# Moving the reload of a residual stream and the loads of a post-processing in a fused two-layer encoder

## The chip, the cores and the metric

The kernel runs on one core of a Trainium2 chip. The metric is the device time of one execution in microseconds (us); smaller is better. A core has several engines that run their own instruction streams side by side and wait for each other by semaphores: TensorE (PE: matmuls; PEld: the loading of their weights), VectorE (DVE), ScalarE (ACT, "Activation"), GpSimd (POOL), and SyncE (SP), which here only issues transfers. Transfers between the chip's memory and the on-chip buffers are issued by SP and by ACT, each on a queue of its own and in its own program's order; 16 DMA engines carry them. Float32 is used throughout, and each large product is computed as three products of a high and a low part.

## What is computed

The reference is a stream of 1024 positions of width 1024 through two layers, each followed by a SwiGLU feed-forward block, with a last RMS norm:

```python
def reference(x, ...):
    h = x
    for layer in range(DEPTH):
        hn = rms_norm(h, mix_norm[layer])
        if layer % 2 == 0:
            h = h + hybrid_ab_mixer(hn, ...)
        else:
            y, v_first = rwkv7_time_mix(hn, ...)
            h = h + y
        h = h + swiglu(rms_norm(h, ffn_norm[layer]), ffn_w_gate[layer], ffn_w_up[layer],
                       ffn_w_down[layer])
    return rms_norm(h, final_norm)

def swiglu(hn, w_gate, w_up, w_down):
    return (jax.nn.silu(hn @ w_gate) * (hn @ w_up)) @ w_down
```

The second layer's mixer, `rwkv7_time_mix`, projects the stream to r, k, v, a decay and a gate g, runs a recurrence over time for 16 heads of 64 channels, and ends with a post-processing: a group norm of the recurrence's result y, a bonus term that multiplies v, and the gate:

```python
    y = wkv7_scan(rh, decay, kh, vh, -kk, kk * ah)
    mean = jnp.mean(y, axis=-1, keepdims=True)
    var = jnp.mean(jnp.square(y - mean), axis=-1, keepdims=True)
    y = ((y - mean) * lax.rsqrt(var + GN_EPS)).reshape(bsz, seq, d)
    y = y * ln_w.astype(f32) + ln_b.astype(f32)
    bonus = jnp.sum(rh * kh * r_k.astype(f32), axis=-1, keepdims=True) * vh
    y = (y + bonus.reshape(bsz, seq, d)).astype(h.dtype)
    return (y * g) @ w_o, v_first
```

The recurrence is computed in chunks of 64 positions, whose triangular systems are inverted beforehand.

## The kernel before

The sequence is worked on in two halves of 512 positions (`HT`), h = 0 and h = 1. The residual stream of a half is a tile `H[h]` of 128 x 8 x 512 values (2 MB): channels on the partitions in 8 blocks. Memory on the chip is short, so `H[h]` is written to DRAM (`h_d`) and loaded again when the half's turn comes.

**Weights.** `plan` lists all weight tiles of 512 KB in the order in which they are taken. `take(key)` (L133) hands out the next one, counts it in `pos[0]`, has the next two loaded by `load_at` (L108, the issue on ACT's queue at L115) and the next one split by `split` (L144: ACT copies the high part, L145, and DVE subtracts for the low part, L146). Three raw tiles are buffered.

**The two mixed stages.** In each half's turn there is a stage in which the recurrence of one half, `recur` (L1144), runs beside the feed-forward block of the other, `ffn` (L647). Both are generators; `drive` (L731) runs the dense one, earns `RATIO` = 3.0 units for each weight (one eighth of a weight at a time) and spends them on steps of the recurrence, each of which names its cost as it yields. The steps are traced at a priority raised by `AHEAD` = 450 instructions; a scheduler then puts each engine's instructions into a fixed order, by priority and by when it takes them to be ready. So the place of an instruction in the code isn't its place in its engine's stream. `tc.issue_after(i)` draws an edge: what is traced under it stands behind i on i's engine. It adds an order, not a semaphore wait.

**The recurrence's loads.** `load(c)` (L1181) loads what chunk c needs, on SP's queue: `ar` and `bk` (512 KB each), the values `uv`, and the inverses `XT` (L1195, L1198) from `xi_d`, which the stage before has written (L1126). Chunks 0 and 1 are loaded at the start; `burst(c)` (L1269) loads chunk c + 2 at its end. `gram` (L1203) makes the products of `ar` and `bk`, which DVE evicts (L1215); `below`, `below2` and `own` go on with them (evictions L1241, L1255, L1256, L1266), and the state's steps follow. After each second chunk `post(jj)` (L1328) does the post-processing of 128 positions: it loads the gate `gch` (L1332, 512 KB) and the values `vch` (L1335, two loads of 256 KB) on SP's queue, multiplies the values by the bonus (L1341), takes the statistics, normalizes (L1362), applies weight and bonus (L1367, L1368), transposes, applies bias and gate (L1382) and writes the result to `y_d` (L1386). `gch`, `vch` and the rest have one buffer each. Their loads may be scheduled as soon as the buffer is free, long before the steps that use them.

**The residual's reload.** In a mixed stage `with_reload` (L1468) wraps `recur`: while it passes on the recurrence's first four steps it issues the four pieces of the residual (two channel blocks, 512 KB each) on SP's queue (L1474). They are first needed at the first down projection, whose results DVE adds to `H[h]` (L423).

Of the kernel before, what the change touches and what calls it, by code (L numbers as in the profile page):

```python
# [16 lines left out]
P = 128  # L17
D = 1024
T = 1024
KT = D // P  # L20
# [18 lines left out]
def tile_trunk(  # L39
# [8 lines left out]
    act, dve, pool, pe, sp = nc.scalar, nc.vector, nc.gpsimd, nc.tensor, nc.sync  # L48
# [25 lines left out]
    def bc(ap, shape):  # L74
        return ap.to_broadcast(shape)
# [20 lines left out]
    def col(c):  # L96
        return vec[:, c : c + 1]
# [3 lines left out]
    plan, raws, ready, pos = [], {}, {}, [0]  # L101

    acts, dests, splits = set(), {}, {}

    def push(key, parts, view=lambda t: t, dest=None):
        plan.append((key, parts, view, dest))

    def load_at(i):  # L108
        if i >= len(plan) or i in raws:
            return  # L110
        if plan[i][0][0] in acts and plan[i][0][0] not in dests:
            return
        raw = wst.tile([P, D], F32, tag="raw", name="raw")
        for dst, src in plan[i][1]:
            act.dma_start(dst(raw), src)  # L115
        raws[i] = raw

    def whl():
# [197 lines left out]
    H = [hA, hB]  # L316
# [8 lines left out]
    def pst(tag):  # L325
        t, n = psum["tags"][tag]
        return psum["pool"].tile([P, HT], F32, tag=t, bufs=n, name=t)
# [12 lines left out]
    def hsl(h):  # L340
        return slice(h * HT, (h + 1) * HT)
# [6 lines left out]
    def rsqrt(t):  # L348
        pool.tensor_tensor(out=t, in0=t, in1=mhalf[:, : t.shape[1]], op=ALU.pow)  # L349
# [149 lines left out]
    for h in range(2):  # L499
        ops = [mmt() for _ in range(4)]  # L500
        for kp in range(4):
# [4 lines left out]
            for kk in range(2):  # L506
                k = 2 * kp + kk
# [60 lines left out]
    for m in ORD_Z:  # L568
# [4 lines left out]
        for h in range(2):  # L573
# [16 lines left out]
            while w < win:  # L590
                n = l0.tile([P, 16 + HT], F32, tag="zw", bufs=2, name="zw")
                b0 = base + w
# [23 lines left out]
    for h in range(2):  # L616
        hi, lo = act_tiles((xlp, actp)[h])
        ys.append((hi, lo))
        for k in (4, 5, 6, 7, 0, 1, 2, 3):
            src = zt[k - 4, h] if k >= 4 else mx[:, k, hsl(h)]  # L620
# [133 lines left out]
    v_d = [dram.tile([HT, 2, 8, 64], F32, name=f"v_d{h}") for h in range(2)]  # L754
    bon_d = [dram.tile([4, P, 2, 8], F32, name=f"bon_d{h}") for h in range(2)]
    g_d = [dram.tile([P, KT, HT], F32, name=f"g_d{h}") for h in range(2)]
    xi_d = [dram.tile([2, 8, 2, 8, 32, 2, 32], F32, name=f"xi_d{h}") for h in range(2)]
# [31 lines left out]
    rows = [slice(0, 64), slice(64, 128)]  # L789
# [354 lines left out]
    def recur(h, wp):  # L1144
# [5 lines left out]
        def wt(tag, bufs, shape):  # L1150
            return wp.tile(shape, F32, tag=tag, bufs=bufs, name=tag)
# [5 lines left out]
        for r in range(2):  # L1157
            act.dma_start(
                lnw[rows[r]], rwkv_ln_w[0].rearrange("(p r d) -> r p d", r=2, d=64)[r].partition_broadcast(64)
            )  # L1160
        C, ypair = {}, {}
        S, Q, last = [state_d], {}, []

        def ordered(f, *args, **kw):

            if last:
                with tc.issue_after(last.pop()):
                    i = f(*args, **kw)  # L1168
            else:
                i = f(*args, **kw)  # L1170
            last.append(i.ins)
# [9 lines left out]
        def load(c):  # L1181
            ar = wt("ar", 2, [P, 8, 2, 64])
            sp.dma_start(ar, ar_d[h][c])
            bk = wt("bk", 1, [P, 8, 2, 64])
            sp.dma_start(bk, bk_d[h][c])
            uv = wt("uv", 2, [P, 8, 2, 64])
            vs = v_d[h][c * 64 : c * 64 + 64]
            sp.dma_start(uv[64:128, :, 0, :], vs[:, 0])
            sp.dma_start(uv[0:64, :, 1, :], vs[:, 1])

            xx = wt("XT", 2, [P, 8, 96])
            x1, XT = xx[:, :, 0:32], xx[:, :, 32:96]
            for r in range(2):
                b0 = r * 64
                sp.dma_start(  # L1195
                    xx[b0 : b0 + 32, :, 0:64], xi_d[h][0, :, r, c].rearrange("p i a j -> i p (a j)")
                )
                sp.dma_start(XT[b0 + 32 : b0 + 64, :, 32:64], xi_d[h][1, :, r, c, :, 1].rearrange("p i j -> i p j"))  # L1198
                pool.memset(XT[b0 + 32 : b0 + 64, :, 0:32], 0.0)
            gt = wt("gt", 2, [P, 8, 2, P])  # L1200
            C[c] = (ar, bk, uv, gt, x1, XT)

        def gram(c, q):  # L1203
            ar, bk, _, gt, _, _ = C[c]
            og = [pst("sm").rearrange("p (a b) -> p a b", b=P) for _ in range(2)]
            for j in range(4):
                p = q * 4 + j
                for b in range(2):
                    for r in range(2):
                        mm(  # L1210
                            og[r][rows[b], j, :], bk[rows[r], p, b, :],
                            ar[rows[r], p].rearrange("p a b -> p (a b)"), start=True, stop=True,
                        )
            for r in range(2):
                dve.tensor_tensor(  # L1215
                    out=gt[:, q * 4 : q * 4 + 4, r, :], in0=og[r], in1=bc(gm.unsqueeze(1), [P, 4, P]), op=ALU.mult
                )
# [110 lines left out]
        def post(jj):  # L1328
            yp = ypair[0]
            j = h * 4 + jj  # L1330
            gch = wt("gch", 1, [P, 8, P])
            sp.dma_start(gch, g_d[h][:, :, jj * P : (jj + 1) * P])  # L1332
            vch = wt("vch", 1, [P, 2, 8, 64])
            for r in range(2):
                sp.dma_start(  # L1335
                    vch[rows[r]].rearrange("t c p d -> t c (p d)"),
                    v_d[h][jj * P : (jj + 1) * P, r].rearrange("(c t) p d -> t c (p d)", t=64),
                )
            v16 = vch.rearrange("t c p d -> t (c p) d")
            b16 = bon[:, 2 * j : 2 * j + 2, :].rearrange("t c p -> t (c p)")  # L1340
            pool.tensor_tensor(out=v16, in0=v16, in1=bc(b16.unsqueeze(2), [P, 16, 64]), op=ALU.mult)  # L1341
            st = wt("st", 1, [P, 2, 8, 6])
            for r in range(2):
                for p in range(8):
                    dve.bn_stats(out=st[:, r, p, :], in_=yp[:, r, p, :])
            sts = st.rearrange("p a b s -> p (a b) s")
            mean, dm, var = (wt(n, 1, [P, 16]) for n in ("mean", "dm", "var"))
            me, mo, ve, vo = (sts[:, :, i] for i in (1, 4, 2, 5))
            dve.tensor_tensor(out=mean, in0=me, in1=mo, op=ALU.add)
            dve.tensor_tensor(out=dm, in0=me, in1=mo, op=ALU.subtract)  # L1350
            dve.tensor_tensor(out=var, in0=ve, in1=vo, op=ALU.add)
            dve.scalar_tensor_tensor(out=dm, in0=dm, scalar=16.0, in1=dm, op0=ALU.mult, op1=ALU.mult)
            dve.tensor_tensor(out=var, in0=var, in1=dm, op=ALU.add)
            dve.tensor_scalar(out=var, in0=var, scalar1=1.0 / 64, scalar2=GN_EPS, op0=ALU.mult, op1=ALU.add)
            rsqrt(var)
            dve.scalar_tensor_tensor(out=mean, in0=mean, scalar=-0.5, in1=var, op0=ALU.mult, op1=ALU.mult)
            yield 0.3
            ysb = wt("ysb", 1, [P, 2, 8, 64])
            for r in range(2):
                for p in range(8):  # L1360
                    i = r * 8 + p
                    act.activation(  # L1362
                        ysb[:, r, p, :], yp[:, r, p, :], AF.Identity, scale=var[:, i : i + 1], bias=mean[:, i : i + 1]
                    )
            yield 0.3
            for q, eng in enumerate((dve, pool)):
                eng.tensor_tensor(out=ysb[:, q], in0=ysb[:, q], in1=lnw, op=ALU.mult)  # L1367
                eng.tensor_tensor(out=ysb[:, q], in0=ysb[:, q], in1=vch[:, q], op=ALU.add)  # L1368
            yield 0.3
            yield 0.3  # L1370
            for q in range(2):
                o = pst("sm")
                for i in range(4):
                    p = 4 * q + i // 2 * 2
                    ordered(
                        pe.transpose, o[:, i * P : (i + 1) * P], ysb[:, i % 2, p : p + 2, :].rearrange("t p d -> t (p d)"), ident
                    )
                ov = o.rearrange("p (q c r t) -> p q r c t", q=2, c=2, r=2)
                for i in range(4):
                    m = q * 4 + i  # L1380
                    g = gch[:, m, :].rearrange("p (c t) -> p c t", c=2)
                    dve.scalar_tensor_tensor(  # L1382
                        out=g, in0=ov[:, i // 2, i % 2], scalar=col(C_LNB + m), in1=g, op0=ALU.add, op1=ALU.mult,
                    )
                yield 0.5
            sp.dma_start(y_d[h][:, :, jj * P : (jj + 1) * P], gch)  # L1386

        load(0)
        load(1)
        yield 0.2  # L1390
# [77 lines left out]
    def with_reload(pool_, h, src, side):  # L1468

        H[h] = pool_.tile([P, KT, HT], F32, tag="h", name="h")  # L1470
        k = 0
        for cost in side:
            if k < KT:
                sp.dma_start(H[h][:, k : k + 2, :], src[:, k : k + 2, :])  # L1474
                k += 2
            yield cost


# [145 lines left out]
```

## Time and profile before

| what | us |
|---|---|
| median of 3 runs | 2526.85 (2522.3 to 2532.54) |
| profiled execution, own time | 2537.24 |
| its span, first to last instruction | 2535.5 |
| mean granted clock of TensorE | 0.981 of full speed |
| first mixed stage, loads of chunk 0 to the last post-processing's store | 944.58 to 1209.61 |
| second mixed stage, the same | 1690.54 to 1951.07 |

The profile is of one execution. Its page gives the busy time of each engine and the costliest groups of instructions; from the trace behind it one can ask for the timeline of an engine, for waits with what released them, for the chain of waits that ended last, for busy time, granted clock and DMA load in stretches of time, and for the transfers of a queue. "L345" is line 345 of the kernel. Times count from the start of the span. An engine "SPq" or "ACTq" is a transfer being issued on that queue, not the transfer itself. A releaser is inferred from the order of events, so among several awaited things the last one is named. Matmuls are pipelined: their listed durations overlap, and the distance of two starts tells their pace.

### The profile page before, as it was taken

The numbers are of one execution on the slowest core, as the hardware profiler recorded it, in microseconds if no ns is written. First come the engines' busy times: TensorE is split into PE (matmuls) and PEld (weight loads), VectorE is DVE, ScalarE is ACT, GpSimd is POOL, SyncE is SP. The second block draws the span as 40 slices with busy tenths as digits, with TensorE's granted clock in tenths as the row PEclk, the third lists the DMA queues.
The fourth block names the chain that finished last, engine by engine and source line by source line (L and its number), as shares of the span: only waits on it lengthen the run. The fifth ranks groups of instructions, "written<-read, shape, count | busy, mean of one in ns | idle before, by whom it ended". The sixth has DMA issues, their size and how long they took to land.

```text
span 2535.5 us, 37947 instructions
## 1 busy us (share of the span) xinstructions
PE 2443.4 (96%) x15735; PEld 1985.9 (78%) x15735; DVE 1401.2 (55%) x2118; ACT 889.8 (35%) x1335; POOL 298.9 (12%) x298
## 2 busy tenths in 40 slices
PE   8999999999989998999999999899999999999998
PEld 6888888888767776888877677677888878888887
DVE  5446534444865874655457855965654455534443
ACT  6333322222544432333224543432333223322223
POOL 0200000000323400121002222300211000100001
PEclk9999999999989999999999999999999999999999
DMA  5123434323255477533334355585553332423331
GB/s 180 42 60 99 133 109 123 92 92 117 81 156 134 129 204 193 144 104 101 116 119 135 107 180 129 135 222 159 157 149 108 109 100 84 149 83 115 101 92 58
DMA packets 434956, 310.69 MB, mean 123 GB/s; under 512 B 93216, under 2 KB 395424, under 8 KB 433760
## 3 DMA queue, kind: packets, MB, share of 16 engines
q10 hardware_dynamic: 297280, 210.53, 27.9%
q1 hardware_dynamic: 137504, 97.75, 13.7%
q8 instruction: 123, 2.02, 0.3%
q14 instruction: 49, 0.40, 0.1%
HBM read 254.68 MB, written 53.54 MB: 122 GB/s over the span
## 4 chain that ended last, share of the span: by engine, by line
PE 76%; DVE 10%; DMA 8%; ACT 2%; issue 2%; POOL 1%; ACTq 0%; SPq 0%; DVEq 0%; POOLq 0%
PE mm L345 21%; PE mm L344 21%; PE mm L346 21%; PE sm L1168 5%; DVE wlo L146 2%; DMA raw<-in_ffn_w_up_dram 2%; PE yp L1168 1%; DVE mix L887 1%; DVE it L1117 1%; DMA lnw<-in_rwkv_ln_w_dram 1%; DMA raw<-in_ffn_w_down_dram 1%; DVE xi L1122 1%; DMA raw<-n_d 1%; ACT whi L145 1%; DMA raw<-y_d 1%
## 5 line engine op out<-in xcount | busy, mean ns | idle before, releaser
L345 PE MATMUL mm<-alo,whi 128*128 128x512 f32 x1952 | 773.8, 396 | 1.6 <-DVE alo L146 1.6
L344 PE MATMUL mm<-ahi,whi 128*128 128x512 f32 x1952 | 769.0, 395 | 5.0 <-DVE h L423 4.0
L346 PE MATMUL mm<-ahi,wlo 128*128 128x512 f32 x1952 | 767.7, 393 | 2.6 <-DVE wlo L146 2.6
L145 ACT ACTIVATE whi<-raw 128x1024 fp32r<-128x1024 f32 x288 | 304.3, 1058 | 779.5 <-PE mm L345 606.9
L146 DVE TENSOR_TENSOR wlo<-raw,whi 128x1024 fp32r<-128x1024 f32 x288 | 361.4, 1255 | 313.6 <-ACT whi L145 302.7
L344 PEld LDWEIGHTS mm<-ahi,whi 128*128 128x128 f32 x1952 | 368.1, 189 | 92.0 <-issue 4.6
L345 PEld LDWEIGHTS mm<-alo,whi 128*128 128x128 f32 x1952 | 368.7, 189 | 83.7 <-issue 3.7
L346 PEld LDWEIGHTS mm<-ahi,wlo 128*128 128x128 f32 x1952 | 369.0, 189 | 83.2 <-DVE wlo L146 3.4
L345 PE MATMUL mm<-hidlo,wdhi 128*128 128x512 f32 x624 | 248.1, 398 | 1.2 <-DVE hidlo L672 1.2
L344 PE MATMUL mm<-hidhi,wdhi 128*128 128x512 f32 x624 | 240.5, 395 | 6.7 <-ACT hidhi L671 5.5
L346 PE MATMUL mm<-hidhi,wdlo 128*128 128x512 f32 x624 | 246.9, 396 | 0.0
L423 DVE TENSOR_TENSOR h<-h,mm 128x512 f32<-128x512 f32 x192 | 129.6, 686 | 153.8 <-PE mm L346 153.0
L145 ACT ACTIVATE wdhi<-raw 128x1024 fp32r<-128x1024 f32 x82 | 86.6, 1059 | 258.1 <-DMA raw<-in_ffn_w_down_dram 155.2
L146 DVE TENSOR_TENSOR wdlo<-raw,wdhi 128x1024 fp32r<-128x1024 f32 x82 | 101.1, 1234 | 114.6 <-ACT wdhi L145 114.6
L668 DVE TENSOR_TENSOR sg<-sg,mm 128x512 f32<-128x512 f32 x88 | 60.3, 686 | 168.5 <-PE mm L346 168.1
L344 PEld LDWEIGHTS mm<-hidhi,wdhi 128*128 128x128 f32 x624 | 117.8, 189 | 35.0 <-ACT hidhi L671 7.7
L345 PEld LDWEIGHTS mm<-hidlo,wdhi 128*128 128x128 f32 x624 | 119.1, 191 | 28.7 <-DVE hidlo L672 3.2
L346 PEld LDWEIGHTS mm<-hidhi,wdlo 128*128 128x128 f32 x624 | 118.7, 190 | 24.7 <-issue 0.2
L423 DVE TENSOR_TENSOR hA<-hA,mm 128x512 f32<-128x512 f32 x72 | 48.8, 686 | 78.0 <-PE mm L346 78.0
L349 POOL TENSOR_TENSOR nrs<-nrs,small 128x4 f32<-128x4 f32 x8 | 10.0, 1246 | 627.3 <-DVE nrs L371 627.3
L344 PE MATMUL mm<-xhi,whi 128*128 128x512 f32 (+1 forms) x160 | 65.6, 410 | 4.2 <-ACT k L925 4.2
L672 DVE TENSOR_TENSOR hidlo<-sg,hidhi 128x512 fp32r<-128x512 f32 x88 | 65.7, 746 | 3.8 <-ACT hidhi L671 3.7
(300 smaller groups left out, 2948.0 us busy)
## 6 DMA issues: line engine op xcount, KB each, us to landing
raw<-in_ffn_w_gate_dram ACTq DMA_DIRECT2D x88, 512.0 KB
raw<-in_ffn_w_up_dram ACTq DMA_DIRECT2D x88, 512.0 KB
raw<-in_ffn_w_down_dram ACTq DMA_DIRECT2D x88, 512.0 KB
raw<-in_ab_w_in_dram ACTq DMA_DIRECT2D x16, 512.0 KB
raw<-in_ab_w_out_dram ACTq DMA_DIRECT2D x16, 512.0 KB
raw<-in_rwkv_w_k_dram ACTq DMA_DIRECT2D x16, 512.0 KB
raw<-in_rwkv_w_r_dram ACTq DMA_DIRECT2D x16, 512.0 KB
ar_d<-ar SPq DMA_DIRECT2D x16, 512.0 KB
```

The source lines that it names most:

```text
L145: act.activation(hi, src, AF.Copy)
L146: (eng or dve).tensor_tensor(out=lo, in0=src, in1=hi.bitcast(F32), op=ALU.subtract)
L344: pe.matmul(o, whi, xhi, start=first, stop=False)
L345: pe.matmul(o, whi, xlo, start=False, stop=False)
L346: pe.matmul(o, wlo, xhi, start=False, stop=last)
L423: dve.tensor_tensor(out=H[h][:, m, :], in0=H[h][:, m, :], in1=o, op=ALU.add)
L668: dve.tensor_tensor(out=s, in0=s, in1=o, op=ALU.mult)
L672: dve.tensor_tensor(out=lo, in0=s, in1=hi.bitcast(F32), op=ALU.subtract)
L887: dve.scalar_tensor_tensor(out=t, in0=hn1[:, k, 0:HT], scalar=col(c), in1=t, op0=ALU.mult, op1=ALU.add)
L1117: dve.tensor_tensor(out=t, in0=bc(iat[:, j, j + 1 : 32].unsqueeze(2), sh), in1=bc(xi[:, j, 0 : j + 1].unsqueeze(1), sh), op=ALU.mult,)
L1122: dve.tensor_tensor(out=xs, in0=xs, in1=t, op=ALU.add)
L1168: i = f(*args, **kw)
```

## The change

Two things are moved; nothing is computed otherwise, and the same bytes are loaded.

The residual's pieces in `with_reload` go to ACT's queue. A piece is issued only when a new weight has been taken since the piece before (or since the stage's start), and under an edge behind the weight load issued last (`loaded[0]`, which `load_at` now records).

In `post(jj)` the load of the gate gets an edge behind the last `XT` load of a later chunk (`issued[c]`, which `load` now records): chunk 2, 4, 6 and 7 for jj = 0, 1, 2 and 3. The two loads of the values get an edge behind the load of the gate.

```diff
+    loaded = [None]
...
         for dst, src in plan[i][1]:
-            act.dma_start(dst(raw), src)
+            loaded[0] = act.dma_start(dst(raw), src).ins
...
-        C, ypair = {}, {}
+        C, ypair, issued = {}, {}, {}
...
-                sp.dma_start(XT[b0 + 32 : b0 + 64, :, 32:64], xi_d[h][1, :, r, c, :, 1].rearrange("p i j -> i p j"))
+                i = sp.dma_start(XT[b0 + 32 : b0 + 64, :, 32:64], xi_d[h][1, :, r, c, :, 1].rearrange("p i j -> i p j"))
                 pool.memset(XT[b0 + 32 : b0 + 64, :, 0:32], 0.0)
             gt = wt("gt", 2, [P, 8, 2, P])
             C[c] = (ar, bk, uv, gt, x1, XT)
+            issued[c] = i.ins
...
             gch = wt("gch", 1, [P, 8, P])
-            sp.dma_start(gch, g_d[h][:, :, jj * P : (jj + 1) * P])
+            with tc.issue_after(issued[min(2 * jj + 2, 7)]):
+                vload = sp.dma_start(gch, g_d[h][:, :, jj * P : (jj + 1) * P]).ins
             vch = wt("vch", 1, [P, 2, 8, 64])
             for r in range(2):
-                sp.dma_start(
-                    vch[rows[r]].rearrange("t c p d -> t c (p d)"),
-                    v_d[h][jj * P : (jj + 1) * P, r].rearrange("(c t) p d -> t c (p d)", t=64),
-                )
+                with tc.issue_after(vload):
+                    sp.dma_start(
+                        vch[rows[r]].rearrange("t c p d -> t c (p d)"),
+                        v_d[h][jj * P : (jj + 1) * P, r].rearrange("(c t) p d -> t c (p d)", t=64),
+                    )
...
         H[h] = pool_.tile([P, KT, HT], F32, tag="h", name="h")
-        k = 0
+        k, at = 0, pos[0]
         for cost in side:
-            if k < KT:
-                sp.dma_start(H[h][:, k : k + 2, :], src[:, k : k + 2, :])
-                k += 2
+            if k < KT and pos[0] > at:
+                with tc.issue_after(loaded[0]):
+                    act.dma_start(H[h][:, k : k + 2, :], src[:, k : k + 2, :])
+                k, at = k + 2, pos[0]
             yield cost
```

## The prediction

> **What bounds the kernel now.** I read the page first.
>
> ```profile
> span 2535.5 us, 37947 instructions
> PE 2443.4 (96%) x15735; PEld 1985.9 (78%) x15735; DVE 1401.2 (55%) x2118; ACT 889.8 (35%) x1335; POOL 298.9 (12%) x298
> ```
>
> TensorE sets the end. No matmul is added or removed, so the change can only win from the 92.1 us in which PE is idle, and from matmuls at a low clock. The edits lie in the two stages in which a recurrence runs beside a SwiGLU. There I read the waits of PE in the timeline (start, duration, and in brackets the idle time and what ended it), then the windows over the first such stage (start and end, length, busy time of PE, PEld, DVE, ACT and POOL with counts, then granted clock, DMA share, GB/s).
>
> ```profile
> 968.68 1.10 PE L1168 MATMUL sm<-ar,bk 64*64 64x128 f32 x30 [4.00 <-DVE gt L1215]
> 992.74 0.69 PE L1168 MATMUL sm<-ar,bk 64*64 64x128 f32 x2 [5.04 <-DVE XT L1256]
> 1054.07 0.43 PE L1168 MATMUL sm<-ar,bk 64*64 64x128 f32 x2 [2.19 <-DVE gt L1215]
> 1703.24 0.32 PE L1170 MATMUL sm<-ar,bk 64*64 64x128 f32 x1 [1.31 <-DMA bk<-bk_d]
> 1713.29 1.49 PE L1168 MATMUL sm<-ar,bk 64*64 64x128 f32 x30 [2.85 <-DVE gt L1215]
> 1735.02 0.69 PE L1168 MATMUL sm<-ar,bk 64*64 64x128 f32 x2 [2.84 <-DVE XT L1256]
> ```
>
> ```profile
> 946.00:956.00 10.00, 10.00 (x46) 8.18 (x45) 3.35 (x4) 2.61 (x3) 0.00 (x0) 1.00 1.03 267
> 966.00:976.00 10.00, 7.32 (x53) 6.07 (x54) 4.35 (x5) 3.37 (x4) 0.00 (x0) 0.83 1.11 289
> 986.00:996.00 10.00, 4.96 (x72) 4.00 (x69) 3.13 (x5) 1.91 (x3) 1.90 (x1) 0.71 0.58 165
> ```
>
> Each stage has an **early stall** (968.68; 1703.24 and 1713.29) and a **late stall** (992.74; 1735.02). The DMA share is about 1 or more while they build up: the engines of the DMA are full. The chain of waits gives the reason.
>
> ```profile
> 967.44 6.27 DMA XT<-xi_d
> 973.78 15.29 DMA raw<-in_ffn_w_up_dram
> 989.09 1.06 ACT whi L145
> 992.26 0.43 DVE XT L1256
> 1718.26 13.08 DMA raw<-in_ffn_w_up_dram
> ```
>
> This is a relay: a landing at 973.71 (967.44 + 6.27) lets a weight load of ACT's queue go out at 973.78. So issues wait for landings, not for data alone. That load takes 15.29 us (13.08 in the other stage); its split (989.09) and the eviction behind it (992.26) release PE at 992.74. What fills the DMA stands on SP's queue.
>
> ```profile
> 933.50 0.60 SPq L1099 DMA_DIRECT2D v_d<-epx  x1
> 943.37 1.12 SPq L1126 DMA_DIRECT2D xi_d<-xi  x2
> 962.92 0.46 SPq L1474 DMA_DIRECT2D h<-h_d  x1
> 968.18 1.81 SPq L1474 DMA_DIRECT2D h<-h_d  x3
> 973.20 0.56 SPq L1332 DMA_DIRECT2D gch<-g_d  x1
> 973.80 1.32 SPq L1335 DMA_DIRECT2D vch<-v_d  x2
> 1000.28 0.45 SPq L1198 DMA_DIRECT2D XT<-xi_d  x1
> ```
>
> ```profile
> h<-h_d SPq DMA_DIRECT2D x4, 512.0 KB
> gch<-g_d SPq DMA_DIRECT2D x1, 512.0 KB
> vch<-v_d SPq DMA_DIRECT2D x2, 256.0 KB
> ```
>
> Three residual pieces, the gate and the values (seven transfers, six of them issued at 968.18 to 975.1) stand with the weight load of 973.78.
>
> **The change, part by part.** *Gate and values.* The first post-processing's three loads now go out behind chunk 2's last XT load (1000.28) instead of at 973. They are 1.05 MB; at 289 GB/s that is 3.6 us less for the weight load. Their first user (the gate's, L1382, comes behind it):
>
> ```profile
> 1029.82 0.69 DVE L1368 TENSOR_TENSOR ysb<-ysb,vch 128x512 f32<-128x512 f32 x1
> 1046.34 0.55 SPq L1332 DMA_DIRECT2D gch<-g_d  x1
> 1051.43 0.45 SPq L1198 DMA_DIRECT2D XT<-xi_d  x1
> ```
>
> From 1000.28 to 1029.82 are 29.5 us, so the delay is hidden; if chunk 2's ar and bk, which now follow 1.05 MB, came late, it would cost up to 3.6 us a stage. No semaphore wait is added: it is an order on SP's own queue. For the second post-processing the gate moves from 1046.34 to behind 1051.43, away from the weights before the 2.19 us wait at 1054.07: worth 0 to 2.19 us, I take 1.0. The third moves likewise; the fourth already stands behind chunk 7. These I cost at nothing.
>
> *Residual.* The four loads leave SP for ACT's queue, one to each new weight taken. Counting the generator's costs (0.2, 0.5, 0.5, 2.0, then nine of 0.1 and 6.0, against 0.375 earned per eighth of a weight), the pieces fall into u4, u5, u6 and the first down projection (g and u for gate and up, with the block's number): behind the loads of u5, u6, d4 and g8. SP idles from 934.10 (933.50 + 0.60) to 943.37, yet every load of this stage comes only after the inverse's store: the stage's memory is not free sooner. So the first two pieces cannot go out right behind their weights, whose loads went out before that store; I expect three pieces together on ACT's queue at about 949, behind the small lnw loads, and the fourth behind g8, where three go out now.
>
> *Late stalls.* At 973 the weight load then meets one piece, not three, and no gate or values. It lands at least 3.6 us sooner, and PE comes to that point later (below), so I count both waits as gone: 5.04 + 2.84. The half-speed matmuls behind them go too:
>
> ```profile
> 980.12 0.39 PE L346 MATMUL mm<-ahi,wlo 128*128 128x512 f32 x1
> 981.50 0.39 PE L346 MATMUL mm<-ahi,wlo 128*128 128x512 f32 x1
> 993.35 0.80 PE L345 MATMUL mm<-hidlo,wdhi 128*128 128x512 f32 x1
> 996.08 0.63 PE L345 MATMUL mm<-hidlo,wdhi 128*128 128x512 f32 x1
> 1735.63 0.80 PE L345 MATMUL mm<-hidlo,wdhi 128*128 128x512 f32 x1
> 1738.36 0.63 PE L345 MATMUL mm<-hidlo,wdhi 128*128 128x512 f32 x1
> ```
>
> Seven matmuls start every 0.23 us in the first pair of rows (1.38 / 6), every 0.455 us in the two others (2.73 / 6): 7 x 0.225 = 1.6 us a stage. Late stalls: 5.04 + 2.84 + 3.2 = 11.1 us. What is late next is chunk 1's bk, on the less crowded SP queue.
> [...]
>
> *Early stalls.* They stem from ACT:
>
> ```profile
> 946.12 2.80 ACTq L1158 DMA_DIRECT2D lnw<-in_rwkv_ln_w_dram  x2
> 957.96 0.62 ACT L671 ACTIVATE hidhi<-sg 128x512 fp32r<-128x512 f32 x1
> 965.28 0.39 ACTq L115 DMA_DIRECT2D raw<-in_ffn_w_up_dram  x1
> 965.71 1.06 ACT L145 ACTIVATE wdhi<-raw 128x1024 fp32r<-128x1024 f32 x1 [7.13 <-DMA XT<-xi_d]
> ```
>
> ACT is done at 958.58 and stands until a weight load may go out at 965.28; behind it in order wait a split (965.71), DVE's half of it, and the eviction that releases PE at 968.68. If three pieces (1.57 MB) go ahead of these loads, they cost 1.57 MB / 267 GB/s = 5.9 us; none if they only take SP's place. Below nothing is possible too: were they out of the way, the early stall itself (4.00; 1.31 + 2.85) could go. [...] Four issues more on ACT are 4 x 0.46 us by the row of 962.92; ACT is busy 2.61 of 10 us there, so that is hidden.
> [...]
>
> **Sum:** -11.1 (late) + 6.0 (early) - 1.0 (1054.07) = -6.1 us. The profiled execution took 2537.24 us, of which 1.74 lie around its span; the median of the runs is 2526.85, or 10.4 less, and I carry the saving over in us: **2520.7 us** (-0.24%). With 0 to 5.9 us for each early stall it is 2514.7 to 2526.5.
>
> **Rivals.** *Both stalls go.* If the pieces spread as their order allows, or DVE's eviction is planned ahead of the late split, the early waits of 8.16 us go, and 10 x (1 - 0.83) = 1.7 us of clock twice: 11.6 us. -11.1 - 11.6 - 1.0 gives 2503.2; half of the early part, 2509. For it: the early stall hangs on an order of instructions as much as on bytes. Against: the share of 1.03 before the pieces come.
> *The stall only moves.* The same bytes land by the same time, the early stall takes what the late one gives (5.5 us a stage): 2526.9, at most 3.6 a stage better where gate and values are out of it. [...] For it: shares above 1 from 966 to 976. It is also the case in which the pieces don't spread at all.
> *ACT's queue is held: slower.* A piece that may not go out holds everything behind it on ACT, as 958.58 to 965.28 shows: 6.7 us. If one more such hold per stage comes on top of the 5.9 us of bytes, the early stalls grow by 12.6 each: -11.1 - 1.0 + 25.2 = +13.1, 2540. It is slower at all from 6.05 us growth per stage ((11.1 + 1.0) / 2). For it: PE had no slack left at 964.69. Against: pieces issued at 949 find fewer transfers outstanding.
>
> **How the numbers follow.** Forecast 0.46, both stalls go 0.29, the stall moves 0.16, ACT held 0.09. A measurement tells about 0.5% from no change, here 12.6 us: faster is under 2514.2, slower over 2539.5. Faster: 0.29 and 0.02 from the forecast's lower edge, 0.31; slower 0.09; same 0.60. The range leaves out the held queue and the last of the best case: 2505 to 2532; no unknown of the forecast reaches past it.
>
> **What would show it.** In the changed profile the weight load now at 973.78 takes under 10 us; PE has no wait of over 1 us behind the burst of chunk 0; the granted clock in those windows is 1.00. The residual's four loads stand on ACT, three close together behind lnw; the wait now at 968.68 is some 3 us longer. Gate and values go out after chunk 2's XT. The forecast is wrong if the first pieces go out before the inverse's store, if the early wait shrinks, if ACT stands at an issue for over 7 us, or if chunk 2's products wait for bk.

## The result and the profile after

| | before | after |
|---|---|---|
| median of 6 runs, us | 2527.93 (2522.3 to 2534.86) | 2543.57 (2537.43 to 2549.53) |
| ratio, 95% interval | | 1.0055 (1.0039 to 1.007) |
| profiled execution: span, us | 2535.5 | 2535.7 |

The change is slower by 0.55%, some 14 us, where 0.24% faster was forecast; the time lies above the range. The two profiled spans are equal all the same: the one of before (2537.24 us) ran 9 us over the median above, the one of the change was the shortest of its six. So the traces are compared by their waits, and both kernels were run and profiled once more (below).

The page of the change, its span and its busy times:

```profile
span 2535.7 us, 37949 instructions
PE 2443.1 (96%) x15735; PEld 1986.2 (78%) x15735; DVE 1400.9 (55%) x2118; ACT 890.8 (35%) x1335; POOL 298.6 (12%) x298
```

The work is the same, and TensorE still sets the end. The waits of PE in the two mixed stages on which the reading rests, from its timeline (start, duration, in brackets the idle time and what ended it):

```profile
955.57 0.29 PE L1172 MATMUL sm<-ar,bk 64*64 64x128 f32 x1 [1.28 <-DMA bk<-bk_d]
969.99 0.69 PE L1170 MATMUL sm<-XT,gt 32*32 32x32 f32 x32 [1.35 <-ACT bkt L1229]
983.39 0.43 PE L1170 MATMUL sm<-ar,bk 64*64 64x128 f32 x2 [3.13 <-DVE XT L1259]
1003.40 0.40 PE L1170 MATMUL sm<-ar,bk 64*64 64x128 f32 x2 [1.50 <-DVE Q L1281]
1042.90 0.43 PE L1170 MATMUL sm<-ar,bk 64*64 64x128 f32 x2 [1.63 <-DVE gt L1218]
1056.41 0.40 PE L1170 MATMUL sm<-ar,bk 64*64 64x128 f32 x2 [1.10 <-DVE Q L1281]
1155.20 0.44 PE L1170 MATMUL sm<-XT,gt 32*32 32x32 f32 x16 [3.14 <-issue]
1717.22 0.24 PE L1170 MATMUL sm<-XT,w 32*32 32x32 f32 x2 [2.45 <-ACT w L1244]
1723.66 0.43 PE L1170 MATMUL sm<-ar,bk 64*64 64x128 f32 x2 [1.76 <-DVE XT L1259]
1743.90 0.66 PE L1170 MATMUL sm<-ar,bk 64*64 64x128 f32 x2 [3.56 <-issue]
1789.23 0.43 PE L1170 MATMUL sm<-ar,bk 64*64 64x128 f32 x2 [2.37 <-DVE gt L1218]
1859.57 0.40 PE L1170 MATMUL sm<-ar,bk 64*64 64x128 f32 x2 [1.74 <-DMA bk<-bk_d]
```

The stalls of before have shrunk: the early ones to 1.28 and 1.35 (from 4.00) and 2.45 (from 1.31 and 2.85), the late ones to 3.13 (983.39, from 5.04) and 1.76 (1723.66, from 2.84). New are 1003.40, 1056.41, 1743.90 and 1859.57, 7.9 us together, all ahead of products of `ar` and `bk`, and 1155.20. (Two more that before has not, 1.16 us at 1144.24 and 1.81 at 1870.00, stand behind evictions of ACT and DVE.) For the four before `ar` and `bk` the profile gives three releasers: an eviction of DVE, nothing ("issue"), the landing of `bk`. That the last name holds for all four is read from SP's queue and from the transfers. SP's timeline of the change at chunk 2 of the second stage (start, duration of the issue):

```profile
1730.74 0.43 SPq L1200 DMA_DIRECT2D XT<-xi_d  x1
1731.22 0.56 SPq L1336 DMA_DIRECT2D gch<-g_d  x1
1731.82 1.37 SPq L1340 DMA_DIRECT2D vch<-v_d  x2
1733.92 1.29 SPq L1191 DMA_DIRECT2D uv<-v_d  x1
1735.30 1.24 SPq L1187 DMA_DIRECT2D bk<-bk_d  x1
```

Gate and values stand right behind `XT`, as the edge wants, and so ahead of `uv` and `bk` of the same chunk; its `ar` went out before them. The transfers of 1735 to 1744, in 40 slices (share of the DMA engines busy in tenths, then GB/s):

```profile
DMA  9999999999999999999999998874355200000000
GB/s 278 273 250 259 244 264 256 182 194 160 191 187 174 192 145 154 225 230 238 171 198 233 179 191 182 234 164 99 117 191 137 101 36 36 18 36 18 0 0 0
```

The DMA is full until slice 24, the last bytes move in slice 37, that is until 1735 + 37 x 0.225 = 1743.3, and PE goes on at 1743.90. But for one packet, only SP's queue moved data there. The transfers tell the tiles by the size of their packets: 4096 bytes for `ar` and `bk`, 512 for the gate, 2048 for the post-processing's values, 256 for `uv`. Taking the end of the last 4096-byte packet on SP's queue behind the issue of a `bk`, the times from issue to landing of chunks 2, 4 and 6 are 3.0 to 4.8 us in before's two stages and 3.6 to 8.1 in the change's; and each of the four new waits ended 0.5 to 0.7 us behind such a landing. Where the chain of waits passes there, it has the row itself (start, length, what):

```profile
1851.99 7.44 DMA bk<-bk_d
1859.57 0.40 PE sm L1170 x2
```

The residual went where it was expected. ACT's timeline of the change:

```profile
943.56 3.60 ACTq L1160 DMA_DIRECT2D lnw<-in_rwkv_ln_w_dram  x2
950.48 2.66 ACTq L1480 DMA_DIRECT2D h<-h_d  x3
953.19 0.60 ACT L663 ACTIVATE sg<-mm 128x512 f32<-128x512 f32 x1 [10.51 <-DMA ar<-ar_d]
963.23 1.07 ACTq L117 DMA_DIRECT2D raw<-in_ffn_w_down_dram  x2
965.43 0.60 ACT L663 ACTIVATE sg<-mm 128x512 f32<-128x512 f32 x1 [8.29 <-DMA ar<-ar_d]
971.16 0.60 ACTq L1480 DMA_DIRECT2D h<-h_d  x1
```

Three pieces go out together behind `lnw`, the fourth behind g8. But ACT stands for 10.51 and 8.29 us until these loads may go, and the two down-projection weights behind the pieces go out 19.7 us behind `lnw` (963.23 - 943.56). In before it was 10.4 (956.55 - 946.12 on the same timeline).

### The profile page after: what moved, and what is told of

It reads as the page before. It is cut to its first block, busy times and chain, and to the rows that moved or that the text cites. A ratio compares the mean times of both kernels' runs of the same rounds, so it can differ in the third digit from the quotient of the medians.

```text
span 2535.7 us, 37949 instructions
## 1 busy us (share of the span) xinstructions
PE 2443.1 (96%) x15735; PEld 1986.2 (78%) x15735; DVE 1400.9 (55%) x2118; ACT 890.8 (35%) x1335; POOL 298.6 (12%) x298
## 5 line engine op out<-in xcount | busy, mean ns | idle before, releaser
L663 ACT ACTIVATE sg<-mm 128x512 f32<-128x512 f32 x88 | 51.4, 585 | 49.4 <-DMA ar<-ar_d 28.7
```

The lines of the kernel that those rows point to most:

```text
L663: act.activation(sg[f], o, AF.Silu)
```

## The experiments

**Theory A:** gate and values hold up `bk` of chunks 2, 4 and 6. **Theory B:** the pieces make ACT stand, and the weights behind them come late. **Rival C:** the edits made the scheduler lay the work out in another fixed order, which happens to be worse. "PE's waits" below is the sum of PE's idle times over 0.6 us in the two mixed stages (945 to 1215 and 1690 to 1930 us) of the profiled execution: 20.9 in before, 28.0 in the change. Ratios are to runs of before made beside each group; their medians were between 2530.95 and 2532.48 (15 to 35 runs).

### One part at a time, and both kernels again

The residual alone (the post-processing's loads as before):

```diff
-            with tc.issue_after(issued[min(2 * jj + 2, 7)]):
-                vload = sp.dma_start(gch, g_d[h][:, :, jj * P : (jj + 1) * P]).ins
+            sp.dma_start(gch, g_d[h][:, :, jj * P : (jj + 1) * P])
...
-                with tc.issue_after(vload):
```

> The residual's pieces on Activation's queue as in the change; gate and values loaded as before. Theory A (gate and values now stand ahead of ar, uv and bk of chunks 2, 4 and 6 on SP's queue and make them late): this kernel lacks that, so it is 4 to 8 us faster than before (ratio 0.997 to 0.998). Theory B (three residual pieces at once ahead of the first down weights hold Activation): it carries the whole loss, 12 to 18 us slower (1.005 to 1.007). Theory C (both parts only make the scheduler lay out another fixed order, and that order costs): it differs from before by some amount that is not the change's minus the other part's.

Gate and values alone (the residual as before):

```diff
-            if k < KT and pos[0] > at:
-                with tc.issue_after(loaded[0]):
-                    act.dma_start(H[h][:, k : k + 2, :], src[:, k : k + 2, :])
-                k, at = k + 2, pos[0]
+            if k < KT:
+                sp.dma_start(H[h][:, k : k + 2, :], src[:, k : k + 2, :])
+                k += 2
```

> Gate and values behind the later chunk's XT as in the change; residual on SP's queue as before. Theory A: 12 to 20 us slower than before (1.005 to 1.008), with waits on bk or behind it at the chunks 2, 4 and 6. Theory B: 3 to 8 us faster than before, since 1.05 MB leave the crowd of 973 us. Theory C: its difference and that of the other part alone do not add up to the change's +15 us.

Before and the change, unedited:

> The kernel before, unchanged: ratio 1.000 within its interval. A second profile of it shows which of its PE waits are the same in every execution and which are not; every theory expects the late stalls of 5.0 and 2.8 us again within 1 us.

> The change, unchanged: 1.0055 again, within 1.004 to 1.007. A second profile of it: theory A expects the wait on bk (1.74 us) and the waits of chunks 2, 4 and 6 again, and the two waits named issue (3.1 and 3.6 us) either again or moved; if the waits named issue are larger in slower executions, they carry the spread of 12 us between executions.

| kernel | median us | ratio (95%) | PE's waits | late stalls |
|---|---|---|---|---|
| before again | 2533.05 | 1.0009 (0.9994 to 1.0023) | 21.2 | 1.37, 2.43 |
| the change again | 2549.19 | 1.0065 (1.004 to 1.0089) | 35.1 | 2.83, 3.00 |
| residual alone | 2540.54 | 1.0036 (1.0023 to 1.0049) | 29.8 | 6.09, 6.53 |
| gate and values alone | 2546.23 | 1.0059 (1.0038 to 1.0081) | 31.7 | none |

Each part alone is slower, and they don't add: 0.36 and 0.59 against 0.55 and 0.65 for both. The first late stall of before, 5.04 us in the profile that the prediction read, is 1.37 in the repeat; what the sum counted as a fixed price varies from one execution to the next.

*Gate and values.* The late stalls are gone, as forecast. In their place PE waits six times for `bk` (1.37, 1.36 and 1.62 in the first stage, 2.62, 1.69 and 1.72 in the second): 10.4 us. The repeat of the change shows the same, at its worst in chunk 4. SP's and PE's timeline there:

```profile
1050.21 7.08 SPq L1340 DMA_DIRECT2D vch<-v_d  x2
1059.58 0.57 SPq L1187 DMA_DIRECT2D bk<-bk_d  x1
1066.02 0.65 PE L1170 MATMUL sm<-ar,bk 64*64 64x128 f32 x2 [4.93 <-issue]
```

From the first issue of the values to the end of the second pass 7.08 us: the second goes out at 1056.71, and everything behind it on SP, `uv` and `bk` too, waits with it.

*Residual.* The early stalls shrink from 12.4 us in the repeat of before to 6.4, but the late ones grow from 3.8 to 12.6, and waits for an eviction at 1054.50 and 1794.60 from 1.6 to 7.9: with 0.5 less elsewhere 8.6 us more, which fits the 8 to 9 us of medians and ratio. Counted from `lnw`, PE comes to the first late stall 3.4 us sooner than in the repeat of before and goes on 1.3 us later. The chain of waits into the first late stall (start, length, what):

```profile
976.70 12.13 DMA raw<-in_ffn_w_up_dram
988.86 1.06 ACT whi L147
989.95 0.30 DVE wlo L148
991.20 0.43 DVE XT L1259
991.68 1.32 PE sm L1170 x17
```

It is the late stall of before, with the same links. Between the pieces and the late weights, the windows of the DMA (columns as in the prediction) show a hole, in this kernel and then in the repeat of before:

```profile
965.30:969.30 4.00, 4.00 (x30) 3.22 (x22) 1.29 (x2) 0.40 (x1) 0.00 (x0) 1.00 0.15 49
```

```profile
965.00:969.00 4.00, 4.00 (x19) 3.27 (x18) 0.00 (x0) 0.55 (x1) 0.00 (x0) 1.00 1.16 272
```

With a share of 0.15 the DMA is nearly idle for 4 us; ACT, which stands from 959.80 to 966.83, doesn't send the next weights:

```profile
959.18 0.62 ACT L673 ACTIVATE hidhi<-sg 128x512 fp32r<-128x512 f32 x1
966.83 1.08 ACTq L117 DMA_DIRECT2D raw<-in_ffn_w_down_dram  x2
968.90 0.60 ACT L663 ACTIVATE sg<-mm 128x512 f32<-128x512 f32 x1 [9.10 <-DMA ar<-ar_d]
```

The releaser is a landing on SP's queue, of a tile that ACT doesn't read. The built program has the reason. On ACT, with the counters that each instruction waits for (`DMAHW` and a number: a counter of landings):

```
L1478 DMA h<-h_d 128x1024 [waits DMAHW2]
L663 ACTIVATE sg<-mm 128x512 [waits PE]
...
L117 DMA raw<-in_ffn_w_down_dram 128x1024 [waits DMAHW1,DVE]
```

SP's and ACT's transfers share eight such counters: in the change's trace the 904 issues of both queues use eight semaphores, each of them on both queues, and 526 of them first wait for the one that they use. The load of 966.83 waits for the counter on which SP's load of an `XT`, issued at 958.84, landed at 966.75.

### Moving the cause away

Gate and values behind the later chunk's `bk`, with the residual as before, and then with the residual of the change:

```diff
-            sp.dma_start(bk, bk_d[h][c])
+            issued[c] = sp.dma_start(bk, bk_d[h][c]).ins
...
-            issued[c] = i.ins
```

> The post-processing's gate and values stand behind the later chunk's bk instead of behind its XT; the residual is reloaded as before. Theory A (on SP's queue 1.05 MB of gate and values, half of it in 256-byte packets, stand between a chunk's XT and its bk, so bk of chunks 2, 4 and 6 lands 3 to 4 us later and PE waits for it): none of the six waits of 1.4 to 2.6 us before the products of ar and bk is left, the late stalls at 990 and 1735 stay under 2.5 us, and the time is 2520 to 2532. Rival C (the edit made the scheduler lay the work out in another fixed order, and that order is slower): moving the loads by three places changes little, 2540 to 2548.

> The whole change, but with gate and values behind the later chunk's bk. Theory A: the waits named issue before the products of ar and bk go (13.4 us with the Q waits of the last trace of the change), what is left is the loss of the residual alone, less the gate and values that no longer stand before chunk 1's bk: 2530 to 2540. Rival C: 2543 to 2550, as the change.

The pieces in the order of the change, but on SP; gate and values as before:

```diff
                 with tc.issue_after(loaded[0]):
-                    act.dma_start(H[h][:, k : k + 2, :], src[:, k : k + 2, :])
+                    sp.dma_start(H[h][:, k : k + 2, :], src[:, k : k + 2, :])
```

> The residual's pieces behind the weight loads in the order of issue, but issued on SP; gate and values as before. Theory B (on ACT the three pieces, and the two down-projection loads behind them, wait for landings of SP's loads, so that ACT stands for 10.5 and 9.1 us and these weights go out 8.7 us later, which comes back as the late stalls of 6.09 and 6.53 us): the two loads go out again within 13 us of lnw, the late stalls are 5 us or less, and the time is 2528 to 2536. Rival (the pieces' place in the order costs, whoever issues them): 2538 to 2543, with late stalls over 6 us.

Only the values behind `XT`, the gate behind `bk`; residual as before:

```diff
-            with tc.issue_after(issued[min(2 * jj + 2, 7)]):
-                vload = sp.dma_start(gch, g_d[h][:, :, jj * P : (jj + 1) * P]).ins
+            with tc.issue_after(issued[min(2 * jj + 2, 7), 1]):
+                sp.dma_start(gch, g_d[h][:, :, jj * P : (jj + 1) * P])
...
-                with tc.issue_after(vload):
+                with tc.issue_after(issued[min(2 * jj + 2, 7)]):
```

(`issued[c, 1]` is the load of `bk`, `issued[c]` that of `XT`.)

> Residual as before. Only the values (0.52 MB in 256-byte packets) stand behind the later chunk's XT, the gate (0.52 MB in 512-byte packets) behind its bk. Theory A with the packets deciding (many small packets hold bk): most of the loss stays, 2538 to 2546. A with the bytes deciding: half of it, 2534 to 2540. C: as the whole post-processing moved, 2543 to 2549.

| kernel | median us | ratio (95%) | PE's waits | late stalls |
|---|---|---|---|---|
| gate, values behind bk | 2530.97 | 1.0002 (0.9988 to 1.0017) | 17.6 | none |
| the same, pieces on ACT | 2532.72 | 1.0004 (0.9991 to 1.0017) | 21.1 | 3.12, 2.10 |
| pieces on SP | 2531.19 | 0.9991 (0.9978 to 1.0005) | 20.8 | 4.14, none |
| values behind XT, gate behind bk | 2524.01 | 0.9963 (0.9949 to 0.9977) | 15.5 | none |

Behind `bk` no wait for `bk` of chunks 2, 4 and 6 is left; these land 3.3 to 4.1 us behind their issue, as in before, and the whole loss of gate and values is gone. That settles A, and C can be read from the traces. Compared one by one (operation, tiles, shape), all 2118 instructions of DVE, 1335 of ACT and 298 of POOL come in the same order with gate and values behind `XT` alone and behind `bk` alone, and again in the change and in the change with both behind `bk`; so do PE's 15735 matmuls but for 4 and 6 places, where two traces of before itself differ in 8. What differs is SP's stream. So another fixed order is not what makes gate and values slow.

The second pair also says more than A asked: with the pieces still on ACT the change comes from 1.0055 and 1.0065 down to 1.0004. Behind `bk` the residual on ACT costs nothing (1.0004 against 1.0002), so its 0.36% is no fixed price of ACT's queue; it hangs on where gate and values stand.

On SP the two down-projection weights go out 12.1 us behind `lnw` (956.40 - 944.26) and the residual costs nothing. That takes the loss away together with ACT, but not with ACT's queue alone: with the pieces on SP the order on DVE, ACT and POOL is that of before, and with the pieces on ACT some 120 of DVE's and 90 of ACT's instructions stand elsewhere. For the residual C is not ruled out. But A gives no gain over before, although both late stalls went: the profiled span was 11 us shorter than that of the repeat of before, the medians are equal. A wait like the one that the change brought at 1155.20 (3.14 us) stays late in the first stage, 2.51 us here and 2.03 with the pieces on ACT, and its cause is not settled. And with the values alone behind `XT` all expectations fell, to the better side. Their premise was off too: the 256-byte packets that they give the values are those of `uv`; the values go in 2048-byte packets, a quarter as many as the gate's.

### Half the bytes, and combinations

The mirror of the last kernel (the gate behind `XT`, the values behind `bk`):

```diff
             with tc.issue_after(issued[min(2 * jj + 2, 7)]):
-                vload = sp.dma_start(gch, g_d[h][:, :, jj * P : (jj + 1) * P]).ins
+                sp.dma_start(gch, g_d[h][:, :, jj * P : (jj + 1) * P])
...
-                with tc.issue_after(vload):
+                with tc.issue_after(issued[min(2 * jj + 2, 7), 1]):
```

> The mirror of the run with the values behind XT: residual as before, only the gate (0.52 MB) behind the later chunk's XT, the values behind its bk. If bk has slack for 0.52 MB and not for 1.05 MB (what the time of 2524.0 with the values alone suggests), then no wait for bk is over 1 us in chunks 2, 4 and 6 and the time is 2522 to 2532. If it is the gate that holds bk and not the values, 2536 to 2546.

The values behind `XT` and the gate behind `bk`, with the pieces on SP; with the pieces on ACT; and once more with the residual as before:

> The best parts together: the pieces behind the weight loads but issued on SP, the values behind the later chunk's XT, the gate behind its bk. If the parts add: ratio 0.996 to 0.994 to before, 2517 to 2525. If the late stalls are what both parts save: 2522 to 2528, no better than the values alone.

> The whole change, with the gate alone taken behind the later chunk's bk. Theory A and B: no waits for bk of chunks 2, 4 and 6, but the three pieces on ACT still send the down-projection weights out some 20 us behind lnw, with late stalls of 2 to 3 us a stage: 2528 to 2537, slower than the same with the residual as before (2524.0) by 4 us or more. If the place of gate and values were all of the loss: 2522 to 2527.

> The kernel that was fastest so far, once more: ratio 0.995 to 0.998 to before, if its gain of 0.37% is more than a good draw.

| kernel | median us | ratio (95%) | PE's waits | late stalls |
|---|---|---|---|---|
| gate behind XT | 2525.57 | 0.9974 (0.9958 to 0.9989) | 18.2 | none |
| values behind XT, pieces on SP | 2521.26 | 0.9955 (0.994 to 0.997) | 19.7 | none |
| values behind XT, pieces on ACT | 2529.95 | 0.9999 (0.9984 to 1.0014) | 17.2 | 1.58, 3.04 |
| values behind XT again | 2521.36 | 0.996 (0.9946 to 0.9974) | 14.2 | none |

Either half may stand ahead of `bk`, both may not, and it is the bytes and not the number of packets that the two halves share. 0.52 MB is within what `bk` can wait but for a single wait of 1.36 us in the first run of the values and 1.91 us with the pieces on SP; 1.05 MB isn't. With the gate ahead `bk` still lands 5.3 to 7.6 us behind its issue, nearly as late as with both, yet PE waits for it only 0.98 and 0.93 us; so the last microsecond or two seems to be what costs. The gain of 0.4% repeats. The same kernel with the pieces on ACT is 0.4% slower, 8.6 us, about what the residual alone cost (2529.95 against 2521.36), where behind `bk` it cost nothing. With the pieces on ACT the order on DVE, ACT and POOL is that of the change; in the other three kernels it is that of before but for 2, 3 and 6 instructions.

### What on ACT does it

Four loads of 2 KB in ACT's order where the change has the pieces, with everything else as before (nothing reads them):

```diff
+            if n < 4 and pos[0] > at:
+                with tc.issue_after(loaded[0]):
+                    act.dma_start(scr[:, 4 * n : 4 * n + 4], src[:, 2 * n, 0:4])
+                n, at = n + 1, pos[0]
```

> Residual, gate and values as before, but four more loads of 128x4 elements (2 KB each, into a tile that nothing reads) stand in ACT's order where the change has the residual's pieces. By waits (each load that ACT issues first waits for a landing, so ACT stands whatever the size): the two down-projection loads go out 18 us or more behind lnw, as with the pieces (20.6), against 11.9 before, and the time is 2536 to 2543. By bytes: they go out within 14 us, and the time is 2529 to 2535.

The residual alone on ACT in two pieces of 1.05 MB; it is also run a second time:

```diff
-                    act.dma_start(H[h][:, k : k + 2, :], src[:, k : k + 2, :])
-                k, at = k + 2, pos[0]
+                    act.dma_start(H[h][:, k : k + 4, :], src[:, k : k + 4, :])
+                k, at = k + 4, pos[0]
```

> The residual alone on ACT, gate and values as before, in two pieces of 1.05 MB in place of four of 0.52. By bytes: as the four pieces, 2538 to 2543, late stalls of 6 us. By waits: one wait less ahead of the down-projection loads, which go out 2 us or more sooner than 20.6 us behind lnw, and 2533 to 2539.

> The two pieces once more: ratio 0.994 to 0.998 to before, if the gain of 0.42% is more than a good draw.

Four pieces at once on ACT, none later:

```diff
-            if k < KT and pos[0] > at:
-                with tc.issue_after(loaded[0]):
-                    act.dma_start(H[h][:, k : k + 2, :], src[:, k : k + 2, :])
-                k, at = k + 2, pos[0]
+            if k < KT:
+                act.dma_start(H[h][:, k : k + 2, :], src[:, k : k + 2, :])
+                k += 2
```

> The residual alone on ACT, in four pieces of 0.52 MB issued one after the other behind lnw, none later; gate and values as before. If the late fourth piece is what costs (it joins the crowd at 976): as the two pieces, 2518 to 2526, late stalls under 2 us. If the number of loads on ACT costs: as the four of the change, 2536 to 2543, late stalls over 5 us.

The two pieces with the values behind `XT` and the gate behind `bk`:

> Two pieces on ACT, values behind the later chunk's XT, gate behind its bk. If the two gains add (0.42% and 0.38%): 2509 to 2516. If both only take away the late stalls: 2517 to 2524.

| kernel | median us | ratio (95%) | PE's waits | late stalls |
|---|---|---|---|---|
| four loads of 2 KB | 2532.17 | 0.9998 (0.9986 to 1.0009) | 20.2 | none |
| two pieces | 2520.67 | 0.9958 (0.9944 to 0.9972) | 14.0 | none |
| two pieces again | 2524.1 | 0.9965 (0.995 to 0.998) | 15.5 | none |
| four pieces at once | 2544.48 | 1.005 (1.0031 to 1.0068) | 29.1 | 8.72, 8.50 |
| two pieces, values behind XT | 2531.65 | 0.9997 (0.9983 to 1.001) | 15.2 | none |

Neither form of B stands as it was put. The count without the bytes is free. The same bytes at the same place cost 0.5% in four loads and win 0.4% in two: 20 to 24 us between them. ACT's timeline with four at once, then its waits with two (from its list of waits, us in total, times, longest):

```profile
954.01 7.21 ACTq L1477 DMA_DIRECT2D h<-h_d  x4
961.26 0.60 ACT L663 ACTIVATE sg<-mm 128x512 f32<-128x512 f32 x1 [15.11 <-DMA uv<-v_d]
974.59 0.60 ACT L663 ACTIVATE sg<-mm 128x512 f32<-128x512 f32 x1 [9.36 <-DMA raw<-in_ffn_w_down_dram]
```

```profile
ACT hidhi L673 <- DMA uv<-v_d: 9.0, 1, 9.0
ACT sg L663 <- DMA lnw<-in_rwkv_ln_w_dram: 8.7, 1, 8.7
```

24.5 us of standing against 17.7. But the down-projection weights go out equally late (20.6 and 19.9 us behind `lnw`), and so does the load on which the late stall hangs, the second of an up-projection behind `lnw`: 32.1 us with four at once and 30.4 with the four of the residual alone, 31.6 in both runs of the two. What differs is how long it takes, and when gate and values go out on SP. Four at once (the second row is from the chain of waits), then two:

```profile
976.58 0.56 SPq L1335 DMA_DIRECT2D gch<-g_d  x1
979.16 10.72 DMA raw<-in_ffn_w_up_dram
```

```profile
968.00 0.57 SPq L1335 DMA_DIRECT2D gch<-g_d  x1
974.43 0.40 ACTq L117 DMA_DIRECT2D raw<-in_ffn_w_up_dram  x1
981.39 1.06 ACT L147 ACTIVATE whi<-raw 128x1024 fp32r<-128x1024 f32 x1 [1.44 <-DMA raw<-in_ffn_w_up_dram]
```

In both stages of both kernels with two pieces the gate goes out 6.4 to 7.2 us ahead of this load, which is split 6.4 to 7.9 us behind its issue; in both with four it goes out 2.3 to 3.0 us ahead, and the split comes 10.7 to 12.2 us behind. So the late stall is again the crowd of before, gate and values beside this weight. That fits the other kernels too: with gate and values moved, four pieces (2529.95) and two (2531.65) are alike. It is a reading of the traces and no experiment: what lets the gate out sooner with two is not settled, and the two kernels also differ in the place of some 50 instructions each on DVE and ACT. Why the pieces on ACT, two or four, cost 0.4% against the values behind `XT` alone (2521.36) is open as well: PE's waits are as few (15.2), and of the 7 us that the first stage takes longer than in the second run of the two pieces, instruction against instruction, waits explain 2.

The best kernels are the values behind `XT` with the pieces on SP (0.9955), two pieces on ACT (0.9958 and 0.9965), and the values behind `XT` alone (0.9963 and 0.996). Their intervals overlap.

## Why the prediction was wrong

*The step that failed: "so the delay is hidden".* Gate and values were priced by their own first use, 29.5 us later, and by what they take out of the way of ACT's weight. What they stand in front of was seen, "if chunk 2's ar and bk, which now follow 1.05 MB, came late, it would cost up to 3.6 us a stage", and left out of the sum; the third and fourth post-processing I costed "at nothing". Alone the part costs 0.59%, some 15 us, of which 10.4 are six waits for `bk`: 4.4 and 6.0 us a stage, more than the bound, since chunks 4 and 6 wait as chunk 2 does. `bk` has one buffer, where `ar` has two, so its load can't go out early; that is in the code, and should have made `bk` the first thing to ask for. (No run gives `bk` a second buffer.) That their place is the cause is shown by moving them: with gate and values behind `bk` the change's whole loss is gone (1.0004).

*Late stalls, "I count both waits as gone".* With gate and values moved and the residual left on SP they are gone. In the change 4.89 of 7.88 us stay. "Meets one piece, not three" was right, and the weight's load did take less (7.71 us in the second stage's chain of waits, 13.08 before). "PE comes to that point later" was not: counted from `lnw`, PE goes on 6.8 us sooner at the first late stall, but it also comes there 4.9 us sooner, since the early stall is smaller, and 5.04 - 1.9 leaves 3.13. The half clock behind the stalls was priced at seven matmuls, 1.6 us a stage; in before the windows 1735 to 1738 and 1738 to 1741 both have 0.50, so by an estimate from them it was 3 us in the second stage.

*Early stalls, "+ 6.0 (early)".* Wrong sign: 8.16 us became 5.08 in the first trace of the change. No run shows the 3.0 us a stage that make up this term; what the trace of before has is that SP's queue (q1) moved 2.06 MB and ACT's (q10) 0.83 MB from 966 to 976, at a DMA share of 1.11. Three pieces behind `lnw` did go out together, as said; that they push the two weights behind them, from 10.4 to 19.7 us behind `lnw`, was right in kind. But the early stall doesn't wait for them any more. DVE's timeline of before, then of the change:

```profile
966.80 1.23 DVE L146 TENSOR_TENSOR wdlo<-raw,wdhi 128x1024 fp32r<-128x1024 f32 x1 [6.89 <-ACT wdhi L145]
967.95 1.28 DVE L1215 TENSOR_TENSOR gt<-sm,gm 128x512 f32<-128x512 f32 x2
```

```profile
963.00 1.29 DVE L1218 TENSOR_TENSOR gt<-sm,gm 128x512 f32<-128x512 f32 x2 [2.93 <-PE sm L1170]
969.49 1.23 DVE L148 TENSOR_TENSOR wdlo<-raw,wdhi 128x1024 fp32r<-128x1024 f32 x1 [5.20 <-ACT wdhi L147]
```

In before the split of the late weight stands ahead of the evictions that release PE; in the change the scheduler put the evictions first. The rival "both stalls go" had named this ("DVE's eviction is planned ahead of the late split"); the forecast took the order of before as given.

*The wait of 1054.07, "I take 1.0".* 2.19 became 1.63 (1042.90), and 2.37 came up at 1789.23, where before had nothing over 0.6. No gain.

*The rivals.* "ACT's queue is held" gave 2540 and had 0.09. The residual alone gives that, 2540.54, but the place named was wrong (the early stalls shrank), and so its price fits by chance. The condition was seen, ACT standing from 958.58 to 965.28 in before; I gave it little weight because "pieces issued at 949 find fewer transfers outstanding". They wait all the same, 10.51 us. What had no chance of its own is what decided most: that the moved loads hold up what stands behind them on SP.

*The move to ACT's queue.* The pieces alone gave 1.0036 on ACT and 0.9991 on SP from the same places in the code. On ACT they stand in a stream that also computes and waits for landings (10.51 us in the change), and, as said, in another fixed order.

*The time it was put against.* The 5.04 us stall was read from one execution 9 to 10 us above the median; in the repeat it is 1.37. A sum of -6.1 us was within what one execution differs from the next.

## What to carry to other kernels

When a load is moved on a queue, price first what stands right behind it there, above all a load into a single buffer, which can't be sent ahead; its own first use comes second. Here the queue took some delay for nothing and then cost fast (0.52 MB ahead of `bk`: 0.3 to 0.4% faster; 1.05 MB: 0.6% slower), so move half and measure. When a part is tested alone, test it in the other part's places too: the pieces on ACT cost 0.36% with gate and values as before and nothing with both behind `bk`, and two pieces of 1.05 MB beat four of 0.52 MB by 20 us and more in the first case and not at all with the values behind `XT`. And compare the order of each engine's instructions before a difference is put down to a transfer: an edit that only moves loads can move the scheduler's order with it.

## What the runs showed of the hardware

In the repeat of the change PE's half clock doesn't follow from the length of the last wait alone. Two waits and the 4 us behind each (the last three columns are granted clock, DMA share and GB/s):

```profile
1167.80 0.64 PE L1170 MATMUL sm<-XT,gt 32*32 32x32 f32 x16 [2.26 <-issue]
1738.76 0.43 PE L1170 MATMUL sm<-ar,bk 64*64 64x128 f32 x2 [3.00 <-DVE XT L1259]
```

```profile
1167.80:1171.80 4.00, 4.00 (x24) 3.26 (x25) 0.43 (x1) 0.38 (x1) 1.90 (x1) 0.50 0.01 4
1738.76:1742.76 4.00, 4.00 (x74) 3.25 (x76) 1.37 (x3) 0.00 (x0) 0.00 (x0) 1.00 0.44 126
```

In the 4 us after the wait of 2.26 us the clock was 0.50, in those after the wait of 3.00 us it was 1.00.

A wait that the profile gives to "issue", or to an eviction, ahead of a product of loaded tiles can be a landing: the four new ones of the change there ended 0.5 to 0.7 us behind a landing of `bk`, under three names.
